# Rotary tables, projections, head-norm slices and gate rows set at other places in a two-block transformer kernel

## The chip, the cores and the metric

One core of one Trainium2 chip runs the whole program in one launch. The metric is the device time of that launch in microseconds (us); the time of the kernel before is a median of three runs. TensorE is called PE in the rows, VectorE DVE, ScalarE ACT, GpSimd POOL, and SP is the engine whose queue issues nearly all transfers.

## What is computed

512 tokens of width 1024 pass through two transformer blocks. The first has stick-breaking attention and latent (MLA) softmax attention with rotary positions, eight heads each, and then a mixture of 16,384 tiny experts. The second has a modulation computed from a vector `c` (called ada in the kernel), three kinds of attention heads (six "fox" heads with a forgetting gate, four mLSTM heads, six block-sparse "moba" heads) and a gated feed-forward layer. The parts that the change touches, cut from the reference:

```python
# first block
proj = h @ w_in[l]                      # sb_q, sb_k, sb_v, cq, ckv, k_pe
q = (rms_norm(cq, cq_norm[l]) @ w_uq[l]).reshape(b, s, MLA_HEADS, MLA_QK_DIM)
q = rms_norm(q, q_norm[l]); k = rms_norm(k, k_norm[l])
q = concatenate([q[..., :64], rope(q[..., 64:], positions)])   # cos and sin tables
# second block
mod = silu(c) @ w_ada[l] + b_ada[l]     # six rows: sh1, sc1, g1, sh2, sc2, g2
y_fox  = _fox_attention(_rms(fq, fox_q_g), _rms(fk, fox_k_g), fv, ff + fox_f_bias)
y_moba = _moba_attention(_rms(bq, moba_q_g), _rms(bk, moba_k_g), bv, slopes)
x = x + g1 * (y @ w_out[l])
x = x + g2 * ((silu(gate) * up) @ w_down[l])
```

## The kernel before

Tokens lie in four tiles of 128. Every fp32 product is made of three products of rounded parts ("a triple", `mm3`, lines 329 to 331): a weight tile is loaded on SP's queue (`w`), rounded by ACT (`whi`, line 198), and its remainder taken by DVE, for some weights by POOL (`wlo`, line 200). The stream `W` does this two weight tiles ahead of use: the call `W.get` that opens a weight tile puts the cast and the subtraction of a later tile into the queues of ACT and DVE.

Each engine runs its own list in the order in which the program was written; no scheduler reorders it. So what is written first also stands first in the queue, and a DVE instruction whose input is late holds up all DVE work behind it. The order is made by Python generators. `tok_gen` yields after each triple of a token product (32 triples for a full one), `feat_gen` after each triple of a 128-feature product (8 triples). `beside(main, side)` takes one step of `side` after each triple of `main`. `mix(main, fill)` and `Fill.run` hand out steps of a filler by a credit in ns. `run_pipe` lays out the attention items with lags between scores, transposes and value products, and gives the filler a credit for each item.

In order of time, what the change touches:

- **Tables.** After the products `cq` and `ckv`, DVE computes the rotary tables (lines 670 to 705, one sine on ACT), and then `latent_T` runs beside the product `sbv`: squares on ACT, a Newton inverse root on DVE, scaling, and transposes of `cqk` on PE (line 375).
- **Head norms.** `head_norm_gen` normalises and rotates the MLA queries `m_q` as a filler of the products `ukv` and `sbqk_gen(0)`; then `head_T` transposes them (line 768). The same is done for the keys `m_k` beside `sbqk_gen(1)` and `(2)`; `sbqk_gen(3)` is a filler of the attention.
- **Second block.** `fq` is projected, then `fk` with `fox_q` beside it, then `bq` with `fox_k` beside it. Each of these side generators holds a head norm of 16 steps (12 of the inverse root, 4 multiplications `fx_t`), then some small work, then transposes (line 1421). `moba_heads` does the same for `bq` and `bk`. `cum` is the running sum of the forgetting gates.
- **Ada.** On each `W.get`, one step of `ada_gen` loads a 128x512 piece of `w_ada`, multiplies it on POOL by a column of silu(c) broadcast along the row (lines 642, 644) and adds it (line 645). PE sums such a piece over partitions some steps later (line 633).
- **Gate rows.** `row_from_cols` turns the column form of `g1` and `g2` into rows: eight times DVE builds a diagonal `dg` and PE multiplies it by ones. For `g1r` this stands between the last transposes of `y` and the second half of the output product `out0`; for `g2r` between the last `up` product and the `down` product.

Of the kernel before, what the change touches and what calls it, by code (L numbers as in the profile page):

```python
# [15 lines left out]
OP = mybir.AluOpType  # L16
# [38 lines left out]
OUT_EARLY = 8  # L55

# [102 lines left out]
def build(tc, A, out):  # L159
# [459 lines left out]
    def ada_gen(pool, js):  # L619
# [16 lines left out]
        for i, (j, c) in enumerate(units):  # L636
            load(i + 1)
            w = tiles.pop(i)
            col_ = csil[:, c:c + 1].to_broadcast([P, 512])
            if c == 0:  # L640
                ac = pool.tile([P, 512], F32, name="ada_a", bufs=2)
                nc.gpsimd.tensor_tensor(ac, w, col_, op=OP.mult)
            else:
                nc.gpsimd.tensor_tensor(w, w, col_, op=OP.mult)
                nc.gpsimd.tensor_tensor(ac, ac, w, op=OP.add)
# [25 lines left out]
    nc.vector.memset(chmask[0:64, S - 64:S], NEG)  # L671
    nc.vector.tensor_scalar(utri, jp, 0.0, None, op0=OP.is_ge)
    posf = b1.tile([P, NT], F32, name="posf")
    nc.vector.tensor_copy(posf, posi)
    ang = b1.tile([P, 2, NT, 16], F32, name="ang")
    for tt in range(NT):
        nc.vector.tensor_scalar(ang[:, 0, tt, :], invf, posf[:, tt:tt + 1], None, op0=OP.mult)
    angk = b1.tile([P, 2, NT, 16], F32, name="angk")
    MAGIC = 12582912.0
    i2p = 1.0 / (2.0 * math.pi)  # L680
    nc.vector.tensor_scalar(angk[:, 0], ang[:, 0], i2p, MAGIC, op0=OP.mult, op1=OP.add)
    nc.vector.tensor_scalar(angk[:, 1], ang[:, 0], i2p, 0.25, op0=OP.mult, op1=OP.add)
    nc.vector.tensor_scalar(angk[:, 1], angk[:, 1], MAGIC, None, op0=OP.add)
    nc.vector.tensor_scalar(angk, angk, -MAGIC, None, op0=OP.add)
    nc.vector.tensor_copy(ang[:, 1], ang[:, 0])
    c1 = 6.28125
    c2 = float(np.float32(np.floor((2 * math.pi - c1) * 2 ** 20) / 2 ** 20))
    c3 = float(np.float32(2 * math.pi - c1 - c2))
    for cc in (c1, c2, c3):
        nc.vector.scalar_tensor_tensor(ang, angk, -cc, ang, op0=OP.mult, op1=OP.add)  # L690
    nc.vector.tensor_scalar(ang[:, 1], ang[:, 1], math.pi / 2, None, op0=OP.add)
    PI = 3.1415925
    nc.vector.tensor_scalar(ang, ang, PI, -PI, op0=OP.min, op1=OP.max)
    nc.scalar.activation(ang, ang, AF.Sin)

    trig = []
    for k, g in enumerate((qr, kr)):
        t = b1.tile([P, NT, 4, 16], F32, name="trig%d" % k)
        g1 = g[:, None, 0:16].to_broadcast([P, NT, 16])
        g2 = g[:, None, 16:32].to_broadcast([P, NT, 16])  # L700
        nc.vector.tensor_mul(t[:, :, 0, :], ang[:, 1], g1)
        nc.vector.tensor_mul(t[:, :, 1, :], ang[:, 1], g2)
        nc.vector.tensor_mul(t[:, :, 2, :], ang[:, 0], g2)
        nc.vector.tensor_scalar(t[:, :, 2, :], t[:, :, 2, :], -1.0, None, op0=OP.mult)
        nc.vector.tensor_mul(t[:, :, 3, :], ang[:, 0], g1)
        trig.append(t)

    sbv = b1.tile([P, NT, 512], F32, name="sbv", tag="sbv")
# [1073 lines left out]
```

## Time and profile before

| what | value |
|---|---|
| median of three runs | 2392.91 us (2389.0 to 2395.34) |
| the profiled execution | 2386.05 us, its span 2384.3 us |
| PE busy | 2272.4 us, 95% of the span |
| DVE, ACT, POOL busy | 1603.8, 967.2, 1085.2 us |
| mean granted clock of PE | 0.971 of full speed |

PE is the engine that is busy nearly all the time, so what counts is when it waits and at which clock it runs. A line of the timeline of PE begins with the start in us from the span's start and the duration; where PE was idle before, the idle time and what it waited for stand in brackets at the end. A row of stretches has, for each engine, the busy us and the number of instructions, then the granted clock (1.00 is 2.4 GHz, 0.50 is 1.2 GHz), the share of the transfer engines and GB/s.

### The profile page before, as it was taken

The page shows a single profiled execution, that of the slowest core. Times are in us where ns is not written, and L with a number is a line of the kernel's source. Part 1 is how long each engine was busy: PE and PEld are TensorE (multiplying, and loading weights), DVE is VectorE, ACT ScalarE, POOL GpSimd, SP SyncE. Part 2 cuts the span into 40 slices and gives each one's busy share as a digit, 9 for nine tenths or more (in the row PEclk, how much of TensorE's full clock was granted, in tenths as well). Part 3 has the DMA queues.
Part 4 walks back from the last instruction along what each step waited for, and adds up shares of the span by engine and source line. Part 5 has one row for each costly group of instructions (what it writes and reads, how often), then busy time and mean ns, then how long its engine had stood idle before and what let it go on. Part 6 is the DMA issues. An engine that isn't in the chain of part 4 may idle for free.

```text
span 2384.3 us, 31909 instructions
## 1 busy us (share of the span) xinstructions
PE 2272.4 (95%) x11721; PEld 1948.5 (82%) x11721; DVE 1603.8 (67%) x2979; ACT 967.2 (41%) x1712; POOL 1085.2 (46%) x763
## 2 busy tenths in 40 slices
PE   7899999988989999999999999999799998999999
PEld 7777778878878888888888888888797776888787
DVE  5666639999967788888888877875675355433322
ACT  4556633446763333333333333335454434222211
POOL 4460024645766666776667666643656102500000
PEclk9998999999999999999999999999899899999999
DMA  5430042325688888998989888962342112423231
GB/s 169 137 115 1 11 154 88 104 96 197 238 292 304 306 303 298 319 313 310 331 306 320 307 307 306 317 235 90 128 131 93 45 36 71 158 92 98 85 112 56
DMA packets 174936, 439.91 MB, mean 184 GB/s; under 512 B 16956, under 2 KB 71100, under 8 KB 171708
## 3 DMA queue, kind: packets, MB, share of 16 engines
q1 hardware_dynamic: 136188, 301.28, 37.6%
q0 software_dynamic: 36864, 134.23, 15.5%
q10 hardware_dynamic: 1728, 2.36, 0.3%
q8 instruction: 92, 1.51, 0.3%
q14 instruction: 64, 0.52, 0.1%
HBM read 406.10 MB, written 31.72 MB: 184 GB/s over the span
## 4 chain that ended last, share of the span: by engine, by line
PE 70%; DVE 15%; issue 5%; POOL 4%; ACT 3%; DMA 2%; SPq 0%; ACTq 0%; POOLq 0%; DVEq 0%
PE bank L331 20%; PE bank L329 20%; PE bank L330 20%; DVE ohAB L1114 3%; DVE ohA L1121 3%; PE bank L571 2%; POOL rows L1241 2%; PE bank L582 2%; POOL wlo L200 2%; PE bank L563 1%; DVE wlo L200 1%; DMA w<-in_uT_dram 1%; PE bank L811 1%; DVE eq L1054 1%; DMA w<-in_peer_v_dram 1%
## 5 line engine op out<-in xcount | busy, mean ns | idle before, releaser
L200 POOL TENSOR_TENSOR wlo<-w,whi 128x1024 fp32r<-128x1024 f32 (+2 forms) x154 | 398.4, 2590 | 416.8 <-ACT whi L198 367.9
L331 PE MATMUL bank<-hhi,wlo 128*128 128x384 f32 (+1 forms) x1600 | 576.0, 360 | 11.3 <-POOL wlo L200 10.9
L329 PE MATMUL bank<-hhi,whi 128*128 128x384 f32 (+1 forms) x1600 | 579.7, 362 | 0.7 <-ACT ge L914 0.7
L330 PE MATMUL bank<-hlo,whi 128*128 128x384 f32 (+1 forms) x1600 | 573.3, 358 | 1.4 <-DVE hlo L455 1.4
L198 ACT CAST whi<-w 128x1024 fp32r<-128x1024 f32 (+4 forms) x414 | 420.9, 1024 | 322.2 <-PE bank L331 173.8
L200 DVE TENSOR_TENSOR wlo<-w,whi 128x1024 fp32r<-128x1024 f32 (+2 forms) x260 | 326.9, 1259 | 277.3 <-ACT whi L198 275.4
L331 PEld LDWEIGHTS bank<-hhi,wlo 128*128 128x128 f32 x1600 | 303.5, 190 | 39.2 <-POOL wlo L200 16.3
L329 PEld LDWEIGHTS bank<-hhi,whi 128*128 128x128 f32 x1600 | 303.5, 190 | 34.1 <-issue 4.1
L330 PEld LDWEIGHTS bank<-hlo,whi 128*128 128x128 f32 x1600 | 303.4, 190 | 30.2 <-DVE hlo L455 2.0
L330 PE MATMUL bank<-wlo,ch 128*128 128x512 f32 x768 | 304.7, 397 | 4.5 <-DVE wlo L200 4.4
L329 PE MATMUL bank<-whi,ch 128*128 128x512 f32 x768 | 304.3, 396 | 4.3 <-DMA w<-in_uT_dram 2.8
L331 PE MATMUL bank<-whi,cl 128*128 128x512 f32 x768 | 304.4, 396 | 0.0
L1219 DVE TENSOR_TENSOR cl<-ge,ch 128x384 fp32r<-128x384 f32 x125 | 148.5, 1188 | 140.4 <-ACT ch L1218 139.5
L1241 POOL DMA_INDIRECT rows<-in_peer_v_dram,eidx x128 | 183.2, 1432 | 109.7 <-DVE acc L1264 81.8
L1241 POOL DMA_INDIRECT rows<-in_peer_u_dram,eidx x128 | 178.5, 1394 | 99.6 <-DVE junk L1259 75.3
L1259 DVE SCALAR_TENSOR_TENSOR junk<-rows,h 128x1024 bf16<-128x1024 f32 x128 | 188.3, 1471 | 0.5 <-DMA rows<-in_peer_u_dram,eidx 0.2
L1264 DVE SCALAR_TENSOR_TENSOR acc<-rows,coefg,acc 128x1024 f32<-128x1024 f32 x127 | 181.6, 1430 | 0.7 <-DMA rows<-in_peer_v_dram,eidx 0.4
L330 PEld LDWEIGHTS bank<-wlo,ch 128*128 128x128 f32 x768 | 144.8, 189 | 36.6 <-DVE wlo L200 5.3
L329 PEld LDWEIGHTS bank<-whi,ch 128*128 128x128 f32 x768 | 144.8, 188 | 36.2 <-ACT ch L1212 3.1
L331 PEld LDWEIGHTS bank<-whi,cl 128*128 128x128 f32 x768 | 144.9, 189 | 35.7 <-DVE cl L1219 0.6
L329 PE MATMUL bank<-whi,hhi 128*128 128x384 f32 (+3 forms) x448 | 170.5, 381 | 0.0
L914 ACT ACTIVATE ge<-bank 128x384 f32<-128x384 f32 x116 | 57.1, 493 | 269.8 <-PE bank L331 265.7
(384 smaller groups left out, 3553.5 us busy)
## 6 DMA issues: line engine op xcount, KB each, us to landing
w<-in_uT_dram SPq DMA_DIRECT2D x128, 512.0 KB
w<-in_peer_v_dram SPq DMA_DIRECT2D x128, 512.0 KB
ada_w<-in_w_ada_dram SPq DMA_DIRECT2D x96, 256.0 KB
gdram<-gs SPq DMA_DIRECT2D x24, 1024.0 KB
gblk<-gdram SPq DMA_DIRECT2D x16, 1536.0 KB
w<-in_w_gu_dram SPq DMA_DIRECT2D x44, 512.0 KB
w<-in_w_down_dram SPq DMA_DIRECT2D x22, 512.0 KB
w<-in_w_pq_dram SPq DMA_DIRECT2D x16, 512.0 KB
```

What stands on the lines that cost most here:

```text
L198: nc.scalar.copy(hi[:, :n], t[:, :n])
L200: (eng or nc.vector).tensor_tensor(lo[:, :n], t[:, :n], hi[:, :n].bitcast(F32), op=OP.subtract)
L329: nc.tensor.matmul(o, ah, bh, start=start, stop=False)
L330: nc.tensor.matmul(o, ah, bl, start=False, stop=False)
L331: nc.tensor.matmul(o, al, bh, start=False, stop=stop)
L914: nc.scalar.activation(t, b[:, :DTOK], AF.Gelu)
L1114: nc.vector.tensor_tensor(AB.rearrange("p c b i t -> p (c b) i t"), iota4, IJ[:, n].rearrange("p c (b t) -> p (c b) t", t=2).unsqueeze(2) ...
L1121: nc.vector.tensor_tensor(A[:, c], AB[:, 0], g_, op=OP.mult)
L1219: nc.vector.tensor_sub(cl, t, ch.bitcast(F32))
L1241: nc.gpsimd.indirect_dma_start(out=r, out_offset=None, in_=A["peer_" + kind], in_offset=bass.IndirectOffsetOnAxis(ap=eidx[:, k:k + 1], axi ...
L1259: nc.vector.scalar_tensor_tensor(junk, r, 1.0, h2, op0=OP.mult, op1=OP.mult, accum_out=preg[:, k:k + 1])
L1264: nc.vector.scalar_tensor_tensor(acc, r, coefg[:, k:k + 1], acc, op0=OP.mult, op1=OP.add)
```

## The change

It has five parts. The rotary tables become a generator, `tables()`, and run beside the `cq` product, one step after each triple. `sbqk_gen` can be called for its query or key half alone: the query half of 1 moves in front of the transposes of `m_q`, and the query half of 3 in front of those of `m_k`; within `head_norm_gen`, the rotation uses four instructions over all tokens instead of sixteen. In the second block `SLACK = 6` empty steps stand between the head norms and what follows. `row_from_cols` becomes `row_gen`, whose steps run beside the second half of `out0` for `g1r` and beside the `gate` product of the last but one slice (f = 20) for `g2r`. POOL multiplies in `ada_gen` by a per-partition scalar (`tensor_scalar`) instead of a broadcast tile.

```diff
@@ ada_gen
-            col_ = csil[:, c:c + 1].to_broadcast([P, 512])
+            col_ = csil[:, c:c + 1]
...
-                nc.gpsimd.tensor_tensor(w, w, col_, op=OP.mult)
+                nc.gpsimd.tensor_scalar(w, w, col_, None, op0=OP.mult)
                 nc.gpsimd.tensor_tensor(ac, ac, w, op=OP.add)
@@ tables
-    proj_tok("cq", hhi, hlo, KC, 384, lambda tt, b: nc.scalar.copy(cqk[:, tt, :384], b[:, :384]))
+    def tables():
+        nc.vector.memset(chmask, 0.0)
+        yield
...
+        nc.scalar.activation(ang, ang, AF.Sin)
+        yield
...
+    drain(beside(tok_gen("cq", hhi, hlo, KC, 384, lambda tt, b: nc.scalar.copy(cqk[:, tt, :384], b[:, :384])), tables()))
     proj_tok("ckv", hhi, hlo, KC, 288, ev_ckv)
-
-    nc.vector.memset(chmask, 0.0)
...
@@ sbqk_gen, head_norm_gen
-    def sbqk_gen(j):
+    def sbqk_gen(j, part=(0, 1)):
...
-            for tt in range(NT):
-                nc.vector.tensor_mul(tabs[k][:, tt], s4[:, tt, :, x0:x0 + 16],
-                                     tr[:, tt, k, :][:, None, :].to_broadcast([P, NH, 16]))
-            yield 800.0
+            nc.vector.tensor_mul(tabs[k], s4[:, :, :, x0:x0 + 16],
+                                 tr[:, :, k, :].unsqueeze(2).to_broadcast([P, NT, NH, 16]))
+            yield 700.0
...
     mix(sbqk_gen(0), fill)
+    mix(sbqk_gen(1, (0,)), fill)
     fill.finish()
     fill = Fill(head_norm_gen(ks, trig[1]))
     for tt in range(NT):
         head_T(tt, qs, qg, qhT)
-    mix(sbqk_gen(1), fill, 0.9)
+    mix(sbqk_gen(1, (1,)), fill, 0.9)
     mix(sbqk_gen(2), fill, 0.9)
+    mix(sbqk_gen(3, (0,)), fill, 0.9)
     fill.finish()
...
     def behind():
-        yield from sbqk_gen(3)
+        yield from sbqk_gen(3, (1,))
@@ second block
         def fox_q():
             yield from tq.norm()
+            for _ in range(SLACK):
+                yield
...
             for tt, t in enumerate(tk.t):
                 nc.vector.tensor_scalar(t[:, :, 64], cum[:, tt, 0:6], -8.0, None, op0=OP.mult)
-            yield
+                yield
+            for _ in range(SLACK - 3):
+                yield
             yield from fox_T(tk.t, fkg, kTf)
...
         def moba_heads(heads, gain, dst):
             yield from heads.norm()
+            for _ in range(SLACK):
+                yield
@@ gate rows
+    def row_gen(cols, pool, t):
+        b = dg = None
+        for k in range(9):
+            if k and k % 4 == 0:
+                nc.tensor.matmul(b[:, 384:512], ones, dg, start=True, stop=True)
+                nc.scalar.copy(t[:, (k - 4) * P:k * P], b)
+            elif k:
+                nc.tensor.matmul(b[:, (k - 1) % 4 * P:(k - 1) % 4 * P + P], ones, dg, start=True, stop=True)
+            if k == 8:
+                return
+            if k % 4 == 0:
+                b = bank()
+            dg = pool.tile([P, P], F32, name="dg", bufs=2)
+            nc.vector.tensor_scalar(dg, ident, cols[:, k:k + 1], None, op0=OP.mult)
+            yield
...
-        late_["pool"], late_["g1r"] = b3, row_from_cols(g1c, b3, "g1r")
-        drain(out0)
+        late_["pool"], late_["g1r"] = b3, b3.tile([P, D], F32, name="g1r")
+        drain(beside(out0, row_gen(g1c, b3, late_["g1r"])))
...
-                proj_feat(("gate", f), hhi, hlo, KC, ev_gate)
+                if f == NF - 2:
+                    drain(ada)
+                    W.tick = None
+                    row = row_gen(g2c, b4, g2r)
+                drain(beside(feat_gen(("gate", f), hhi, hlo, KC, ev_gate), row))
                 proj_feat(("up", f), hhi, hlo, KC, ev_up)
-        drain(ada)
-        W.tick = None
-        g2r = row_from_cols(g2c, b4, "g2r")
```

How the instructions move on DVE, at three places. First, behind the norm of the input (`hlo` is the last part of it), where `wlo` belongs to the products `cq` and `ckv` and `ang` to the tables. Before:

```order
L447 SCALAR_TENSOR_TENSOR hlo<-bank,c_attn_norm,hhi 128x512 x8
L200 TENSOR_TENSOR wlo<-w_95,whi 128x768
L200 TENSOR_TENSOR wlo<-w_188,whi 128x576
...
L200 TENSOR_TENSOR wlo<-w_396,whi 128x1024
L670 MEMSET chmask 128x512
...
L705 TENSOR_TENSOR trig_568<-ang,r_k_rope_g 128x4x16
L200 TENSOR_TENSOR wlo<-w_434,whi 128x1024
L335 TENSOR_SCALAR rs_v<-lt_595 128x4
```

The same place now:

```order
L449 SCALAR_TENSOR_TENSOR hlo<-bank,c_attn_norm,hhi 128x512 x8
L673 MEMSET chmask 128x512
...
L684 TENSOR_SCALAR ang<-invf,posf 128x16 x4
L202 TENSOR_TENSOR wlo<-w_95,whi 128x768
...
L703 SCALAR_TENSOR_TENSOR ang<-angk,ang 128x128 x3
L202 TENSOR_TENSOR wlo<-w_188,whi 128x576
...
L725 TENSOR_TENSOR trig_395<-ang,r_k_rope_g 128x4x16
L202 TENSOR_TENSOR wlo<-w_300,whi 128x576
```

The tables, which stood behind seven weight subtractions and in front of the inverse root `rs_v`, now stand between the first subtractions.

Second, beside the `fk` product: `fx_t` are the multiplications of the query norm of the fox heads, `cum` the gates' running sum that the transposes wait for, `hr_ss` the sums of squares of the keys that the product makes. Before:

```order
L1388 TENSOR_TENSOR fx_t<-fx_t,rs_r 128x6x64 x4
L200 TENSOR_TENSOR wlo<-w_15570,whi 128x768
L1443 MEMSET fx_t 128x6 x4
L1449 COPY cum<-bank 128x56
L1367 TENSOR_REDUCE hr_ss<-hr_sq 128x6 x4
```

The same place now:

```order
L1419 TENSOR_TENSOR fx_t<-fx_t,rs_r 128x6x64 x4
L202 TENSOR_TENSOR wlo<-w_15546,whi 128x768
L1398 TENSOR_REDUCE hr_ss<-hr_sq 128x6
L1476 MEMSET fx_t 128x6 x4
L1482 COPY cum<-bank 128x56
L1398 TENSOR_REDUCE hr_ss<-hr_sq 128x6 x3
```

One of the four reductions of the keys has moved in front of the memsets and of `cum`.

Third, where `g1r` is made: `hlo` ends the transposes of `y`, `wlo` belongs to the output product. Before:

```order
L1481 TENSOR_TENSOR hlo<-bank,hhi 128x512 x2
L1338 TENSOR_SCALAR dg<-ident,modc 128x128 x8
L200 TENSOR_TENSOR wlo<-w_17613,whi 128x1024
L200 TENSOR_TENSOR wlo<-w_17881,whi 128x1024
L1635 TENSOR_TENSOR o_t<-bank,g1r 128x512
```

The same place now:

```order
L1518 TENSOR_TENSOR hlo<-bank,hhi 128x512 x2
L202 TENSOR_TENSOR wlo<-w_17589,whi 128x1024
L1371 TENSOR_SCALAR dg<-ident,modc 128x128 x8
L202 TENSOR_TENSOR wlo<-w_17857,whi 128x1024
L1672 TENSOR_TENSOR o_t<-bank,g1r 128x512
```

A weight subtraction, which waits for a cast on ACT, now stands in front of the diagonals.

## Rows read from the trace of the kernel before

**Rows 1.** the page, its first part: busy time of TensorE and its share
```profile
PE 2272.4 (95%) x11721; PEld 1948.5 (82%) x11721; DVE 1603.8 (67%) x2979; ACT 967.2 (41%) x1712; POOL 1085.2 (46%) x763
```

**Rows 2.** timeline of PE: start, us, operation, [idle before <- releaser]
```profile
70.65 1.09 PE L375 MATMUL bank<-ident,cqk 128*128 128x128 f32 x4 [6.32 <-DVE cqk L369]
126.11 5.34 PE L768 MATMUL bank<-ident,m_q 128*96 128x128 f32 x32 [3.48 <-DVE m_q L760]
155.05 3.67 PE L768 MATMUL bank<-ident,m_k 128*96 128x128 f32 x32 [1.61 <-DVE m_k L760]
1690.38 1.09 PE L1421 MATMUL bank<-ident,fx_t 128*65 128x128 f32 x4 [7.88 <-DVE cum L1449]
1716.79 0.62 PE L1421 MATMUL bank<-ident,fx_t 128*65 128x128 f32 x4 [4.38 <-DVE fx_t L1456]
1949.63 4.40 PE L1339 MATMUL bank<-dg,ones 128*128 128x128 f32 x16 [1.75 <-DVE dg L1338]
2023.09 0.50 PE L331 MATMUL bank<-hhi,wlo 128*128 128x512 f32 x1 [2.52 <-POOL wlo L200]
2252.33 0.71 PE L1339 MATMUL bank<-dg,ones 128*128 128x128 f32 x4 [2.36 <-DVE dg L1338]
```

**Rows 3.** busy times by stretch; the granted clock stands behind POOL
```profile
70.00:74.00 4.00, 3.35 (x12) 2.98 (x13) 1.58 (x4) 1.55 (x4) 2.49 (x3) 0.50 0.52 174
180.00:190.00 10.00, 10.00 (x74) 8.53 (x74) 5.59 (x29) 7.48 (x23) 0.00 (x0) 1.00 0.01 2
1717.00:1722.00 5.00, 5.00 (x26) 4.74 (x25) 0.00 (x0) 2.68 (x6) 3.13 (x4) 0.66 0.36 109
2024.00:2032.00 8.00, 8.00 (x37) 6.56 (x36) 2.98 (x4) 1.57 (x2) 6.89 (x6) 1.00 0.83 295
```

**Rows 4.** timelines of DVE, then ACT, around the rotary tables
```profile
52.05 0.48 DVE L670 MEMSET chmask<- 128x512 f32 x1
...
60.18 0.22 DVE L705 TENSOR_TENSOR trig<-ang,r_k_rope_g 128x64 f32<-128x64 f32 x1
...
59.59 0.52 ACT L359 ACTIVATE junk<-cqk 128x384 bf16<-128x384 f32 x1
```

**Rows 5.** timeline of PE: starts of triples in 384- and 512-column products
```profile
35.17 0.34 PE L329 MATMUL bank<-whi,hhi 128*128 128x384 f32 x1
...
35.70 0.34 PE L329 MATMUL bank<-whi,hhi 128*128 128x384 f32 x1
...
52.27 0.39 PE L329 MATMUL bank<-whi,hhi 128*128 128x512 f32 x1
...
52.97 0.40 PE L329 MATMUL bank<-whi,hhi 128*128 128x512 f32 x1
```

**Rows 6.** timeline of DVE: the multiplications of the head norms
```profile
120.35 2.50 DVE L756 TENSOR_TENSOR hn_t<-m_q,trig 128x128 f32<-128x128 f32 x12
...
1684.03 4.46 DVE L1388 TENSOR_TENSOR fx_t<-fx_t,rs_r 128x384 f32<-128x384 f32 x3
...
1709.03 4.76 DVE L1388 TENSOR_TENSOR fx_t<-fx_t,rs_r 128x384 f32<-128x384 f32 x4
...
1747.81 0.56 DVE L1388 TENSOR_TENSOR fx_t<-fx_t,rs_r 128x384 f32<-128x384 f32 x1
```

**Rows 7.** timelines of ACT, DVE and PE around the two gate rows
```profile
1954.55 1.05 ACT L198 CAST whi<-w 128x1024 fp32r<-128x1024 f32 x1
...
1955.63 1.23 DVE L200 TENSOR_TENSOR wlo<-w,whi 128x1024 fp32r<-128x1024 f32 x1 [2.15 <-ACT whi L198]
...
2256.23 0.76 PE L329 MATMUL bank<-whi,ahi 128*128 128x512 f32 x1
```

**Rows 8.** groups of POOL by form: xcount | busy, mean ns | idle before
```profile
L645 POOL TENSOR_TENSOR ada_a<-ada_a,ada_w 128x512 f32<-128x512 f32 x84 | 126.1, 1501 | 6.6
L644 POOL TENSOR_TENSOR ada_w<-ada_w,c_c 128x512 f32<-128x512 f32 x84 | 109.3, 1301 | 125.8 <-DMA ada_w<-in_w_ada_dram 125.5
...
L1352 POOL IOTA dist<- 128x512 f32 x1 | 0.6, 558 | 4.1 <-DVE hlo L455 4.1
```

More of the change, by code (lines that the diff above doesn't have):

```diff
@@ L55 @@
 OUT_EARLY = 8
+SLACK = 6
 NPRE = 4
@@ L678, in build @@
[L678 to L706, printed above, removed]
+    trig = []
@@ L726, in build @@
     qk = {}
-    def sbqk_gen(j):
-        qk[j] = b1.tile([P, 2, S], F32, name="sbqk", tag="qk%d" % j)
-        yield from feat_gen(("sbq", j), hhi, hlo, KC, lambda b: nc.scalar.mul(qk[j][:, 0, :], b, 0.125))
-        yield from feat_gen(("sbk", j), hhi, hlo, KC, lambda b: nc.scalar.copy(qk[j][:, 1, :], b))
+    def sbqk_gen(j, part=(0, 1)):
+        if 0 in part:
+            qk[j] = b1.tile([P, 2, S], F32, name="sbqk", tag="qk%d" % j)
+            yield from feat_gen(("sbq", j), hhi, hlo, KC, lambda b: nc.scalar.mul(qk[j][:, 0, :], b, 0.125))
+        if 1 in part:
+            yield from feat_gen(("sbk", j), hhi, hlo, KC, lambda b: nc.scalar.copy(qk[j][:, 1, :], b))
     qhT = b1.tile([96, NH, S], F32, name="qhT")
@@ L1328, in build @@
     pst.close()
-    def row_from_cols(cols, pool, name):
-        t = pool.tile([P, D], F32, name=name)
-        for hh in range(2):
-            b = bank()
-            for k in range(4):
-                dg = pool.tile([P, P], F32, name="dg", bufs=2)
-                nc.vector.tensor_scalar(dg, ident, cols[:, hh * 4 + k:hh * 4 + k + 1], None, op0=OP.mult)
-                nc.tensor.matmul(b[:, k * P:(k + 1) * P], ones, dg, start=True, stop=True)
-            nc.scalar.copy(t[:, hh * 512:(hh + 1) * 512], b)
-        return t
+    def row_gen(cols, pool, t):
[12 more added lines that the diff above has]
+            nc.vector.tensor_scalar(dg, ident, cols[:, k:k + 1], None, op0=OP.mult)
+            yield
     with tc.tile_pool(name="nrm", bufs=1) as nrm:
@@ L1441, in fox_q @@
             yield from tq.norm()
+            for _ in range(SLACK):
+                yield
             for t in tq.t:
@@ L1456, in fox_k @@
                 nc.vector.tensor_scalar(t[:, :, 64], cum[:, tt, 0:6], -8.0, None, op0=OP.mult)
-            yield
+                yield
+            for _ in range(SLACK - 3):
+                yield
             yield from fox_T(tk.t, fkg, kTf)
@@ L1462, in moba_heads @@
             yield from heads.norm()
+            for _ in range(SLACK):
+                yield
             yield from moba_T(heads.t, gain, dst)
@@ L1684, in build @@
         W.tick = ada_tick
+        row, g2r = iter(()), b4.tile([P, D], F32, name="g2r")
         for f in range(NF):
```

54 lines of the change are left out of this document (46 added, 8 removed).

## The prediction

> **What bounds the kernel now.** I read the busy times first: PE works 95% of the span [rows 1], so a change can gain only where PE stands still, or works at the low clock. The second view was the timeline of PE, searched for idle time above 0.4 us in the stretches that the change touches. The waits that it aims at are seven, and their releasers name the work in front of them [rows 2]: 6.32 us for the scaled latents `cqk`, 3.48 and 1.61 for the rotated queries and keys, 7.88 for `cum` and 4.38 for `fx_t` at the fox heads, 1.75 and 2.36 for the diagonals of the gate rows. They sum to 27.8 us. An eighth, 2.52 us for a `wlo` that POOL makes, stands behind ada work on POOL.
>
> The third view was the granted clock by stretches [rows 3]. Behind the 6.32 us wait PE runs at 0.50, that is 1.2 GHz, for the whole of 70 to 74 us; behind the 4.38 us wait the mean over 5 us is 0.66; behind the 2.52 us wait it is 1.00. So a long wait costs something after its end as well, and one of about 2.5 us need not. Products go at 0.53 us a triple (384 columns) and 0.70 us (512) at 2.4 GHz [rows 5].
>
> **The tables.** DVE spends 52.05 to 60.40 on them, and ACT, which must do the sine in between, starts the squares of the latents at 59.59 [rows 4]. These eight microseconds delay everything that the transposes of `cqk` wait for. Beside `cq` the same instructions stand between weight subtractions that have time: the product lasts 32 x 0.53 = 17 us, and DVE is asked there for 8.4 us of tables and a few subtractions of about 1 us each. If that cover failed, the late subtractions would hold up `cq` or `ckv` by a few us at most, the bound on the bad side. The sine stands in front of the evictions of `cq` on ACT, whose banks are not needed at once. Now the squares can start when the last latent is evicted: about 52.3 by the place where DVE's tables began, and one cast of 1.05 us [rows 7] ahead of them, so 53.3 in place of 59.59, 6.3 us earlier. The transposes would be ready at 70.65 - 6.3 = 64.4; PE reaches them at 70.65 - 6.32 = 64.3. About half a microsecond of wait is left, for a small cast and subtraction that stand in front of the scaling. Gain 5.8 us, and the half-speed stretch goes with it: 4 us at 0.50 are 2.0 us of lost work. Sum 7.8; bounds 4 (2 us of wait left, the clock unchanged) and 8.3.
>
> **The projections.** Eight triples of 0.70 us, 5.6 us, move in front of the transposes of `m_q`. They use finished operands, and the filler of the head norm is fully written out before them, so DVE's end of `m_q` doesn't move; 5.6 covers the 3.48 us. The 32 transposes then last 3.67 us, as for `m_k`, not 5.34 [rows 2]. Gain 5.2. For the keys the number of triples between the two groups of transposes stays 8 + 16 + 8 = 32, so nothing more is hidden there; the four larger rotations instead of sixteen (2.50 us for twelve [rows 6]) may save about 1 us, and transposes that end earlier than their evictions on ACT take about as much back. I put 0 for the keys, between -1.5 and +1.6. The triples taken from the attention's filler are no loss if PE is full there without them: from 180 to 190 us the filler is used up and PE is busy 10.00 of 10 [rows 3]. If it weren't, 5.6 us at most would come back; I take 0.
>
> **The slack.** Six empty steps let PE do six more triples, 6 x 0.53 = 3.2 us, before it asks for the transposes. For the queries that is 1690.38 - 7.88 + 3.2 = 1685.7. DVE is ready at 1690.38 before; now a reduction over 384 columns (about 0.56 us, like a multiplication of that size [rows 6]) stands in front of `cum`, so 1690.9. The wait shrinks from 7.88 to 5.2, a gain of 2.6, and the clock behind it stays low. What makes DVE late is contention: three `fx_t` take 4.46 us where one alone takes 0.56 [rows 6]. POOL runs ada work all that time, at 1.30 us a multiplication and 1.50 an addition [rows 8].
>
> The Trainium skill, "SBUF — State Buffer", section "Who interferes with whom", says that a DVE instruction with two SBUF inputs and a GpSimd instruction that reads SBUF exclude each other, one waiting for the whole of the other. The 4.46 us against 3 x 0.56 agree. By that rule the new POOL multiplication, which reads SBUF too, still locks DVE out, only for a shorter time, so that slack alone can't free the chain.
>
> How long a POOL multiplication by a scalar takes no row shows. The nearest rows are IOTA, 512 columns that are only written, 0.56 us, and the addition with two full inputs, 1.50; the old one took 1.30 [rows 8]. I take 1.0, closer to the old form, whose second input is one column read again and again: 0.3 us less for each of about five DVE instructions that wait behind one here, 1.5 us. The bounds are 5 x 0.74 = 3.7 better and 5 x 0.20 = 1.0 worse. The Trainium skill, "GPSIMD Engine Reference", section "Performance versus the Vector engine", gives 1.03 cycles an element for a body with one input; my estimate from that page is 0.44 us for 512 columns, by which the queries' wait would lose 4.3 us in place of 1.5.
>
> For the keys the wait is 4.38, the steps cover 3.2, and nothing new stands in front: 1.2 is left, short enough to keep the clock, where 5 us at 0.66 lost 1.7 before [rows 3]; I count 1.5 of these. Gain 4.7, bounds 1 and 6.1. The `moba` norms run inside the attention, where no wait of PE names them: 0. Since the steps shift the end of the fox transposes, one more eviction and square on ACT come before the first exponential: -1.
>
> **The gate rows.** `g1r` takes PE from 1949.63 - 1.75 = 1947.9 to about 1954.0 [rows 2], 6.1 us with nothing else. Beside `out0` two triples (1.4 us) come first, and then PE asks for the first `dg`. But the `W.get` in front has put a cast and a subtraction before it: from the cast's start to the end of `wlo` 2.3 us [rows 7]; it can start about 0.6 us after 1947.9, so `dg` is there at 1951.0 and PE has waited 1.8 us since 1949.3. The eight products themselves cost 1.7 us (0.71 us for two at the low clock [rows 2], so about 0.2 each). Gain 6.1 - 1.8 - 1.7 = 2.6. `g2r` takes from 2252.33 - 2.36 = 2249.97 to 2256.23 [rows 2, 7], 6.3 us. Now its first `dg` stands behind the last remainder of `up`, as before, and behind a cast and a subtraction too: I get 2.5 us of wait after two triples, then 1.7. Gain 2.0. Together 4.6; bounds -0.5 (both waits pull the clock down) and 8.7 (no wait). The 2.52 us for POOL's `wlo` has two ada multiplications in front: 0.5, from -0.5 to 2.
>
> **The sum.** 7.8 + 5.2 + 2.6 + 1.5 + 4.7 - 1 + 4.6 + 0.5 = 25.9, say 26 us. The profiled execution took 2386.05 (span 2384.3), so its like would take 2360. It lay 6.9 us under the median of the runs, 2392.91; on the median's scale I predict 2367.
>
> **Rivals.**
> 1. *The waits move with the work.* DVE is in order, so a late DVE chain stays late whatever PE does meanwhile. For it speaks that at the fox queries 5.2 of 7.88 us stay even by my own sum, and that both `dg` get a new wait; against it that tables and projections have their cover on paper. Then tables 7.8 and projections 3.5 hold, the keys of fox give 2, the rest 0: 13 us, 2380.
> 2. *POOL's lock shrinks most of all.* If the multiplication comes near IOTA's 0.56, the queries lose 3.7 instead of 1.5, the keys their last 1.2, the POOL `wlo` 2 and the clock behind the queries returns 1.7: 33 us, 2360.
> 3. *Slower, by POOL.* If the scalar form is slow, ada falls behind. Each `ada_w` piece holds one of two buffers, its load stands in SP's queue in front of the next weight load, and PE waits for weights. The old multiplication has 125.8 us of idle time in front of 84 of them [rows 8], 1.5 us each, so nothing is seen up to 1.3 + 1.5 = 2.8 us. The 26 us are given back at 2.8 + 26/84 = 3.1 us; at 3.4 the loss is 0.6 x 84 = 50 us, net 24 slower, 2417. Against it: it would have to be twice as slow as the addition with two inputs.
> 4. *Nothing in the end.* What PE saves is taken back by stretches at the low clock at other places, where no wait shows: 52 us at 0.50 would do it; 2393.
>
> **How the numbers follow.** Forecast 0.53, rival 1 0.20, rival 2 0.17, rival 3 0.04, rival 4 0.06. No change means within 0.3% of the median, 7.2 us, about what a measurement of this kernel can tell. Cases 0, 1 and 2 are all faster: 0.90, of which I give 0.01 to no change: 0.89, 0.07, 0.04. The range reaches from 39 us gained (rival 2 and the better bounds of the tables and rows) to 11 us gained (rival 1 with a weaker projection term), 2354 to 2382. The spread of the median, 3 us to either side, is in it.
>
> **What would show it.** Right: squares on ACT begin near 53 us, the wait for `cqk` is under 1 us and the clock behind it 1.00; no wait above 1 us before `m_q`, about 1.5 before `m_k`; 4 to 5 us before the first fox transposes of the queries, about 1 before those of the keys; about 2 us in front of the first `dg` of either row, with products following at full speed; POOL's multiplication at about 1.0 us. Wrong: a `cq` or `ckv` triple that waits for `wlo`, gaps in the attention after 165 us, a multiplication on POOL above 2.8 us, or half-speed stretches without a wait in front.

## The result and the profile after

The changed kernel takes 2352.15 us (median of 4 runs, 2348.34 to 2388.42) against 2390.95 us for the kernel before: ratio 0.9828 [0.9802, 0.9854]. Forecast were 2367 us, range 2354 to 2382. The gain is about 39 us by the medians instead of 26 (41 by the ratio, 37 by the ratio of the second comparison below). In some executions, among them the first profiled ones of the changed kernel (2388.42 us) and of the tables put back (2389.76 us), PE runs at 0.50 from about 220 to 300 us and the time is some 35 us longer: ratios leave out executions more than 1.5% above the fastest of their kernel while medians hold all, the rows of the changed kernel are from a second execution (2346.07 us, span 2344.3 us), and those of the tables put back are read only up to 80 us.

The page of that execution, its first part, answers to [rows 1]:

```profile
PE 2256.7 (96%) x11721; PEld 1939.6 (83%) x11721; DVE 1588.4 (68%) x2955; ACT 964.1 (41%) x1712; POOL 1122.6 (48%) x763
```

POOL is busy 37 us longer than before, with the same number of instructions. The timeline of PE at the places of [rows 2], and one wait more (`mlo`, in the first attention) (the line numbers of the changed kernel are its own):

```profile
65.37 0.68 PE L377 MATMUL bank<-ident,cqk 128*128 128x128 f32 x4 [0.66 <-DVE cqk L371]
121.08 3.65 PE L791 MATMUL bank<-ident,m_q 128*96 128x128 f32 x32
147.69 3.67 PE L791 MATMUL bank<-ident,m_k 128*96 128x128 f32 x32 [0.96 <-DVE m_k L783]
218.81 1.45 PE L377 MATMUL bank<-ident,mlo 128*128 128x128 f32 x5 [3.85 <-DVE mlo L371]
1664.33 0.60 PE L1452 MATMUL bank<-ident,fx_t 128*65 128x128 f32 x4
1684.71 0.60 PE L1452 MATMUL bank<-ident,fx_t 128*65 128x128 f32 x4
1914.08 0.46 PE L1365 MATMUL bank<-dg,ones 128*128 128x128 f32 x2 [1.83 <-DVE dg L1371]
1983.71 0.50 PE L333 MATMUL bank<-hhi,wlo 128*128 128x512 f32 x1 [2.51 <-POOL wlo L202]
2194.04 0.49 PE L1365 MATMUL bank<-dg,ones 128*128 128x128 f32 x2 [2.46 <-DVE dg L1371]
```

The reader is to see four things. The waits for `cqk`, `m_k` and both `dg` stand at 0.66, 0.96, 1.83 and 2.46 us, close to the 0.5, 1.6, 1.8 and 2.5 of the forecast. Both fox transposes start without a wait that the timeline shows, where 5.2 and 1.2 us were forecast. And POOL's `wlo` is waited for as long as before. The wait for `mlo` at 218.81 us is new: a gap in the attention after 165 us was one of the signs of being wrong.

The squares of the latents begin where the forecast put them (53.3). Timeline of ACT:

```profile
53.45 0.54 ACT L361 ACTIVATE junk<-cqk 128x384 bf16<-128x384 f32 x1
```

Stretches, with the clock behind POOL, as [rows 3]: behind `cqk`, behind the fox queries, behind POOL's `wlo`:

```profile
66.00:70.00 4.00, 3.71 (x21) 2.75 (x19) 2.43 (x4) 2.86 (x5) 3.48 (x4) 1.00 0.26 94
...
1665.00:1673.00 8.00, 8.00 (x55) 7.73 (x54) 1.66 (x3) 7.35 (x15) 7.45 (x6) 1.00 0.51 164
...
1984.00:1992.00 8.00, 8.00 (x29) 6.40 (x29) 1.43 (x2) 0.61 (x2) 7.48 (x5) 0.79 0.82 266
```

And here is the surprise, the forms of POOL that answer to [rows 8] (xcount | busy, mean ns | idle before):

```profile
L646 POOL TENSOR_SCALAR ada_w<-ada_w,c_c 128x512 f32<-128x512 f32 x84 | 151.6, 1805 | 82.2 <-DMA ada_w<-in_w_ada_dram 81.9
L647 POOL TENSOR_TENSOR ada_a<-ada_a,ada_w 128x512 f32<-128x512 f32 x84 | 114.3, 1361 | 7.0
```

The multiplication became longer, 1.80 us in place of 1.30, and yet the chains on DVE that compete with it became shorter. The multiplications `fx_t` of the head norms, minimum/median/maximum in ns, in the kernel before and then in the changed one:

```profile
L1388 DVE TENSOR_TENSOR fx_t<-fx_t,rs_r x16: 554/1391/1659, 1683.6 to 1780.0; 128x384 f32<-128x384 f32 x16
```

```profile
L1419 DVE TENSOR_TENSOR fx_t<-fx_t,rs_r x16: 545/553/1650, 1659.7 to 1741.6; 128x384 f32<-128x384 f32 x16
```

### The profile page after: what moved, and what is told of

Same layout as the page of the kernel before. It is cut to its first block, busy times and chain, and to the rows that moved or that the text cites. A ratio compares the mean times of both kernels' runs of the same rounds, so it can differ in the third digit from the quotient of the medians.

```text
span 2386.7 us, 31873 instructions
## 1 busy us (share of the span) xinstructions
PE 2295.7 (96%) x11721; PEld 1963.7 (82%) x11721; DVE 1591.5 (67%) x2955; ACT 966.3 (40%) x1712; POOL 1124.4 (47%) x763
## 4 chain that ended last, share of the span: by engine, by line
PE 76%; DVE 12%; issue 3%; ACT 3%; POOL 3%; DMA 2%; SPq 0%; ACTq 0%; POOLq 0%; DVEq 0%
PE bank L331 21%; PE bank L333 21%; PE bank L332 21%; PE bank L573 3%; DVE ohAB L1139 3%; DVE ohA L1146 3%; PE bank L584 2%; POOL rows L1266 2%; PE bank L565 2%; PE bank L836 1%; POOL wlo L202 1%; DMA w<-in_uT_dram 1%; DMA w<-in_peer_v_dram 1%; DVE eq L1079 1%; PE bank L1018 1%
## 5 line engine op out<-in xcount | busy, mean ns | idle before, releaser
L202 DVE TENSOR_TENSOR wlo<-w,whi 128x1024 fp32r<-128x1024 f32 (+2 forms) x260 | 316.2, 1218 | 263.5 <-ACT whi L200 263.3
L646 POOL TENSOR_SCALAR ada_w<-ada_w,c_c 128x512 f32<-128x512 f32 x84 | 151.6, 1804 | 79.1 <-DMA ada_w<-in_w_ada_dram 78.7
```

The costliest lines, as they stand in the source:

```text
L202: (eng or nc.vector).tensor_tensor(lo[:, :n], t[:, :n], hi[:, :n].bitcast(F32), op=OP.subtract)
L646: nc.gpsimd.tensor_scalar(w, w, col_, None, op0=OP.mult)
```

## The experiments

Two theories for the 13 us that were not forecast. A: POOL's scalar form, though longer, holds DVE up less, and the chains at the fox heads are done earlier. B: the clock of PE in the attention, or chance in one of the executions. The table cuts the span at starts of PE's instructions: the norm behind the first attention, the norm that opens the second block, the first 4-row transposes of `mT` (early in the second attention, so that the third stage holds all fox transposes), the last eight value products, the norm behind `out0`. Each number is a difference of two starts, in us.

One execution of each kernel stands in the table, so the scatter must be known. Executions whose program is the same in a stage, those of the later experiments included, gave 316.5 to 319.8 us in the first block, 1286.8 to 1296.8 among the experts, 152.7 to 153.7 from the second block to `mT`, 142.3 to 148.7 in the second attention and 392.2 to 394.8 in the rest. The stage to `mT` is the one in which a difference of a few us can be read from single executions.

| stage | before (two executions) | changed | POOL form back | POOL form alone | no slack | diagonals ahead |
|---|---|---|---|---|---|---|
| first block | 330.9, 331.9 | 318.1 | 322.8 | 328.0 | 316.5 | 319.8 |
| experts | 1296.8, 1290.5 | 1287.1 | 1289.3 | 1288.9 | 1288.5 | 1287.9 |
| second block to `mT` | 168.3, 171.5 | 153.6 | 163.5 | 161.2 | 160.2 | 152.9 |
| second attention | 142.6, 142.7 | 142.8 | 142.7 | 146.6 | 142.6 | 146.6 |
| to the norm behind `out0` | 52.8, 54.1 | 50.5 | 50.5 | 52.8 | 50.5 | 48.5 |
| rest | 392.9, 394.6 | 392.2 | 394.1 | 393.0 | 392.2 | 391.1 |

**The changed kernel again.** No edit.

> The changed kernel itself once more, for a second profile and a closer ratio. Measured so far: 2348 to 2353 us, ratio 0.983, 39 us gained where 26 were summed. Theory A (POOL): the extra gain sits at the fox heads; the wait for the query transposes is gone entirely (5.2 us were expected to stay) because DVE's four fx_t take about 2 us in place of 4.94. Theory B (clock): the extra gain sits in the attention of the first block; this profile then shows 1.00 over most of 210 to 300 us, with under 5 us lost to the low clock where the kernel before lost about 7 (0.62 and 0.52 over 220:240). Ratio 0.981 to 0.985 by either.

Measured: 2350.75 us, ratio 0.9846 [0.9819, 0.9873]. Theory A's picture is there: four `fx_t` in 2.38 us, no wait for the queries. B's is there in part: 0.84 and 0.65 over 210 to 230, some 5 us lost where the kernel before lost about 9 (0.62 and 0.52 from 220 to 240). But the new wait of 3.85 us for `mlo` stands in the same place, so nothing of the 13 us is left for B there.

**POOL's form put back.**

```diff
-            col_ = csil[:, c:c + 1]
+            col_ = csil[:, c:c + 1].to_broadcast([P, 512])
-                nc.gpsimd.tensor_scalar(w, w, col_, None, op0=OP.mult)
+                nc.gpsimd.tensor_tensor(w, w, col_, op=OP.mult)
```

> The changed kernel with one part undone: POOL multiplies by the broadcast column again. Theory A: fx_t on DVE is back at 1.2 to 1.4 us each, the wait before the first query transposes is 4 to 6 us, and the kernel is 6 to 11 us slower than the changed one (ratio to the kernel before 0.986 to 0.989). Theory B: within 3 us of the changed one (0.983 to 0.985). My prediction's own term (1.5 us for this part) lies with theory B here.

Measured: 2363.44 us, 0.9878 [0.985, 0.9907], about 8 us over the changed kernel by the ratios, whose intervals overlap. So the whole does not tell the two kernels apart; the stages do. The waits come back, though the queries' by less than A expected, and one at the MLA keys that nobody had named:

```profile
151.95 4.47 PE L791 MATMUL bank<-ident,m_k 128*96 128x128 f32 x20 [4.24 <-DVE m_k L783]
...
1673.93 1.09 PE L1452 MATMUL bank<-ident,fx_t 128*65 128x128 f32 x4 [2.37 <-DVE fx_t L1476]
1699.44 0.62 PE L1452 MATMUL bank<-ident,fx_t 128*65 128x128 f32 x4 [2.24 <-DVE fx_t L1489]
```

Of the table, 9.9 us lie in the stage to `mT`, ten times its scatter, and 4.6 in the first block (3.0 above the longest of the executions with the changed program), where ada work runs on POOL too. The expected 1.2 to 1.4 us for each `fx_t` failed: their median is 0.61, since the queries' four met POOL at a good moment. It is the whole chain that counts: from `rs_v` to `cum` 12.0 us with this form and slack, 9.4 with the scalar form; in the kernel before 13.4 and 12.5.

**POOL's form alone**, in the kernel before. The same two lines the other way round.

> The kernel before with this part alone: POOL multiplies by a per-partition scalar. Theory A: POOL's multiplication takes 1.55 us or more instead of 1.04 to 1.30, and yet the four fx_t take about 2 us, the 7.88 us wait falls to 4 to 5, the 4.38 us wait to 2 to 3, and the kernel gains 4 to 9 us (ratio 0.996 to 0.998). Theory B: 0 to 2 us (0.999 to 1.000). If the longer multiplication held up ada and through it the weights, it would be slower than before.

Measured: 2371.61 us, 0.9923 [0.9895, 0.995], a gain of 18 us (12 to 25), above what either theory gave. The waits of 7.88 and 4.38 us fall to:

```profile
1674.01 1.09 PE L1421 MATMUL bank<-ident,fx_t 128*65 128x128 f32 x4 [2.43 <-DVE cum L1449]
1697.35 0.62 PE L1421 MATMUL bank<-ident,fx_t 128*65 128x128 f32 x4 [1.42 <-DVE fx_t L1456]
```

The stage to `mT` becomes 8.7 us shorter (against the mean of the two executions before; 7.1 against the shorter of them), the first block 3.4, which is as much as its scatter.

**The pairs by themselves.** Behind the end of the changed kernel: 8 POOL instructions of 512 columns and 16 DVE instructions of 384 columns, alone and together.

```diff
+        for dv, po in ((None, ps), (None, pb), (None, pf), (d2, None), (d1, None),
+                       (d2, ps), (d2, pb), (d2, pf), (d1, ps), (d1, pb), (d1, pf)):
...
+            for i in range(8):
+                if po:
+                    po(i)
+                if dv:
+                    dv(i)
+                    dv(i)
```

> The changed kernel with a measurement added behind its end (so its time is longer by 100 to 200 us and means nothing): 8 POOL instructions of 512 columns alone in each of three forms (scalar, broadcast column, two full inputs), 16 DVE instructions of 384 columns alone (two inputs, one input), then each of the six pairs together. Theory A: the two-input DVE instruction keeps its 0.5 us beside the scalar form, and takes over 1 us beside both others, which exclude it. Theory B, which takes the rule that any POOL instruction reading SBUF excludes it: over 1 us beside all three forms, longest beside the one that lasts longest, the scalar form. One-input DVE instructions: unchanged beside all forms by both.

One line's instructions in each stretch, minimum/median/maximum in ns. L1767 is POOL's scalar form, L1770 the broadcast column, L1773 two full inputs; L1761 is DVE with two inputs, L1764 with one. Where the two engines worked together, only the instructions are counted that ran while the other engine was at work: DVE has 16 of them in a stretch and POOL 8, so a part of either list runs alone. DVE with two inputs alone, then beside L1767, L1770, L1773; with one input the same; POOL's three forms, each alone and then beside L1761:

```profile
L1761 DVE TENSOR_TENSOR mb_dc<-mb_da,mb_db x16: 550/558/559, 2385.3 to 2394.2; 128x384 f32<-128x384 f32 x16
L1761 DVE TENSOR_TENSOR mb_dc<-mb_da,mb_db x14: 557/559/930, 2402.3 to 2411.5; 128x384 f32<-128x384 f32 x14
L1761 DVE TENSOR_TENSOR mb_dc<-mb_da,mb_db x8: 1277/1278/1279, 2418.4 to 2427.5; 128x384 f32<-128x384 f32 x8
L1761 DVE TENSOR_TENSOR mb_dc<-mb_da,mb_db x8: 1499/1499/1501, 2433.6 to 2444.3; 128x384 f32<-128x384 f32 x8
L1764 DVE TENSOR_SCALAR mb_dc<-mb_da x16: 359/360/361, 2394.8 to 2400.7; 128x384 f32<-128x384 f32 x16
L1764 DVE TENSOR_SCALAR mb_dc<-mb_da x14: 359/640/751, 2450.2 to 2458.4; 128x384 f32<-128x384 f32 x14
L1764 DVE TENSOR_SCALAR mb_dc<-mb_da x8: 1078/1082/1083, 2465.2 to 2473.1; 128x384 f32<-128x384 f32 x8
L1764 DVE TENSOR_SCALAR mb_dc<-mb_da x8: 1302/1305/1306, 2477.3 to 2486.7; 128x384 f32<-128x384 f32 x8
L1767 POOL TENSOR_SCALAR mb_pc<-mb_pa,c_c x8: 1562/1562/1584, 2351.0 to 2362.7; 128x512 f32<-128x512 f32 x8
L1767 POOL TENSOR_SCALAR mb_pc<-mb_pa,c_c x5: 1952/1973/1997, 2401.7 to 2409.9; 128x512 f32<-128x512 f32 x5
L1770 POOL TENSOR_TENSOR mb_pc<-mb_pa,c_c x8: 1038/1038/1038, 2364.9 to 2372.7; 128x512 f32<-128x512 f32 x8
L1770 POOL TENSOR_TENSOR mb_pc<-mb_pa,c_c x8: 1232/1235/1444, 2417.8 to 2427.2; 128x512 f32<-128x512 f32 x8
L1773 POOL TENSOR_TENSOR mb_pc<-mb_pa,mb_pb x8: 1259/1262/1262, 2374.4 to 2383.7; 128x512 f32<-128x512 f32 x8
L1773 POOL TENSOR_TENSOR mb_pc<-mb_pa,mb_pb x8: 1455/1456/1675, 2433.0 to 2444.0; 128x512 f32<-128x512 f32 x8
```

This settles it for two inputs. The scalar form is the longest alone (1.56 us against 1.04 and 1.26), but beside it most DVE instructions keep their 0.56: one in three, five of the fourteen, takes 0.85 to 0.93. Beside the other two forms each of the eight takes 1.28 or 1.50, and POOL gets in one instruction for each of DVE's. So a POOL instruction costs DVE about 0.29 us in its scalar form, 0.72 with a broadcast column and 0.94 with two full inputs, while POOL itself becomes longer by 0.41, 0.20 and 0.19. Theory A's "keeps" is not exact, and theory B's order is wrong. What both said of one-input instructions failed: from 0.36 us they go to 1.08 and 1.31 beside the broadcast and the two full inputs, and beside the scalar form two in three are longer, 0.64 and 0.74.

**The kernel before again.** No edit.

> The kernel before, unchanged, for a second profile of it. In the first one the stage of the experts (from the norm behind the first attention to the norm that opens the second block) took 1296.8 us, in the changed kernel and in both variants so far 1287.1 to 1289.3, with the same program in it. Theory A: 8 us of that difference are the scatter of one execution, and the second profile shows 1287 to 1291 there. Theory B: the stage really starts otherwise in the kernel before (order of transfers, clock at entry), and it is above 1294 again.

Measured: 2386.93 us; the experts took 1290.5 us, theory A. In the last experiment below, which holds all of the change, the same stage took 1296.1 us. So it scatters by 9 us and more from one execution to the next, and nothing of it is put down to the change.

**No slack.**

```diff
-SLACK = 6
+SLACK = 0
...
-                yield
-            for _ in range(SLACK - 3):
-                yield
+            yield
```

> The changed kernel without its empty steps between head norms and transposes (SLACK 0, the keys' steps as before). My prediction's terms for the slack are 2.6 us (queries) and 4.7 us (keys). If these stand with POOL's scalar form in place: 5 to 8 us slower than the changed kernel. If POOL's form has already freed DVE, as the kernel before with that form alone shows (waits 2.43 and 1.42 us): 3 to 5 us slower, with waits of about 2.4 and 1.4 us at the fox heads. If DVE's chain sets the end there whatever PE does meanwhile: no difference.

Measured: 2362.38 us, 0.9892 [0.9868, 0.9916], 11.6 us over the changed kernel by the medians, 6.6 us at the fox heads by the table. The waits are 1.77 and 1.66 us, and the clock is 0.50 from 1663 to 1667 and from 1697 to 1701 us, where the changed kernel keeps 1.00 from 1620 us to `mT`:

```profile
1662.62 0.62 PE L1452 MATMUL bank<-ident,fx_t 128*65 128x128 f32 x4 [1.77 <-DVE cum L1482]
...
1686.37 0.62 PE L1452 MATMUL bank<-ident,fx_t 128*65 128x128 f32 x4 [1.66 <-DVE fx_t L1489]
```

**Diagonals four steps ahead.** The products lag, and for `g2r` the diagonals lie in the ring `d_t` over the gate and the up product.

```diff
-        for k in range(9):
+        for k in range(8 + LAG):
+            q = k - LAG
...
+                nc.tensor.matmul(b[:, q % 4 * P:q % 4 * P + P], ones, dgs[q], start=True, stop=True)
```

> The changed kernel with the diagonals of the gate rows built four steps ahead of their products (for the second row in the ring of the last eviction tiles, over the gate and the up product). If the waits of 1.83 and 2.46 us come from the subtraction that stands in front of the first diagonal, as predicted: both gone, 4 us faster than the changed kernel (ratio to the kernel before 0.982 to 0.984). If the diagonals themselves are late on DVE, or the waits only move to the next triple: no difference.

Measured: 2347.79 us, 0.9826 [0.9794, 0.9858]. The wait of `g1r` is gone and the stage shorter by 2.0 us; that of `g2r` is 0.41:

```profile
2198.54 0.49 PE L1366 MATMUL bank<-d_t,ones 128*128 128x128 f32 x2 [0.41 <-DVE d_t L1376]
```

So the subtraction in front of the first diagonal was the reason. As a whole the two kernels are not told apart.

**A gate for `mlo`.**

```diff
...
+        yield lambda: step["k"] >= 41
...
```

> The changed kernel with one gate more in the filler of the first attention: the transposes of the MLA output wait until item 41, not 38 as their norm. If the wait of 3.85 us for mlo is PE asking too early (the filler has 8 triples less than before, so PE gets there sooner): it goes, and with it the stretch at 0.65 to 0.84 behind it; 4 to 8 us faster than the changed kernel. If DVE's chain of items sets the pace of the attention: the wait spreads over the following items and the time stays within 2 us.

Measured: 2349.52 us, 0.984 [0.9815, 0.9865], the wait for `mlo` at 3.85 us as it was. Item 41 was past when the norm was written out, so the order of PE and DVE did not change. This run says nothing of either theory; it is one more measurement of the changed kernel. A later one sets the gate at item 44.

**The tables put back.**

```diff
-    drain(beside(tok_gen("cq", hhi, hlo, KC, 384, ...), tables()))
+    proj_tok("cq", hhi, hlo, KC, 384, ...)
     proj_tok("ckv", hhi, hlo, KC, 288, ev_ckv)
+    drain(tables())
```

> The changed kernel with the rotary tables back behind the second latent product. My prediction's term is 7.8 us (5.8 of wait, 2.0 of half clock behind it); the trace of the changed kernel gives 5.2 to 6 for the wait (from 58.9 to 53.2 to 54.6 us between the first transposes of the input and those of cqk) and 1.5 to 2.4 for the transposes behind it. If the term is right: 6 to 8 us slower than the changed kernel (ratio 0.986 to 0.988), with a wait of 5 to 6 us for cqk. Rival: later stages take up the delay, less than 3 us slower.

Measured: 0.988 [0.9852, 0.9908], against 0.9846 about 8 us, but the intervals overlap. Its profiled execution shows the wait at 4.88 us; up to the end of the `cqk` transposes it needs 4.8 us more than the changed kernel (65.4 and 60.6 us from the first transposes of the input).

**The projections put back.**

```diff
-    mix(sbqk_gen(1, (0,)), fill)
...
-    mix(sbqk_gen(1, (1,)), fill, 0.9)
+    mix(sbqk_gen(1), fill, 0.9)
...
-    mix(sbqk_gen(3, (0,)), fill, 0.9)
...
-        yield from sbqk_gen(3, (1,))
+        yield from sbqk_gen(3)
```

> The changed kernel with the moved halves of the projections put back (the four larger rotations stay). My prediction's term is 5.2 us, all of it at the queries. If it is right: 4 to 7 us slower (ratio 0.986 to 0.988), with a wait of 3 to 4 us for m_q and transposes of 5.3 us instead of 3.7. Rival: the attention has lost filler and waits 3.85 us for mlo, so that half of the gain comes back when the filler does: 0 to 3 us slower, and no wait for mlo.

Measured: 2358.51 us, 0.9909 [0.9866, 0.9952]; the first block takes 322.1 us, 3.9 more than in the changed kernel. `m_q` is waited for 2.81 us, and `mlo` not at all. But the transposes of `m_q` last 3.7 us here, not 5.3. The 3.9 us lie between what the term and what its rival gave (4 to 7, 0 to 3), and 322.1 is only 2.3 above the longest first block of the changed program; the interval of the whole reaches over both. So the run does not decide. Nor is the missing wait for `mlo` a sign for the rival alone: the clock in front of it fell to 0.51 from 210 to 220 us, so PE was slower on the way to it.

**Diagonals ahead, and the gate at item 44.**

```diff
...
+        yield lambda: step["k"] >= 44
...
```

> The changed kernel with the diagonals of the gate rows four steps ahead (as in the run before) and the transposes of mlo held until item 44 of the first attention (item 41 had left the order of PE as it was). If the 3.85 us wait for mlo is PE asking too early: it is gone, the clock stays at 1.00 around 220 us, 4 to 8 us in the first attention and 2 to 4 us at the rows: 2341 to 2346 us, ratio 0.979 to 0.982. If the attention is paced by DVE and ACT: the wait spreads over the items, and 2346 to 2349 us remain.

Measured: 2349.06 us, 0.986 [0.9817, 0.9903]. No wait for `mlo`, and no gain: the first block takes 320.3 us, and the clock in the attention is lower than with the wait. Stretches, the changed kernel and then this one:

```profile
210.00:220.00 10.00, 6.10 (x33) 3.95 (x32) 7.46 (x26) 5.65 (x16) 0.00 (x0) 0.84 0.01 2
220.00:230.00 10.00, 10.00 (x48) 7.26 (x46) 6.62 (x11) 6.47 (x15) 0.00 (x0) 0.65 0.00 0
```

```profile
210.00:220.00 10.00, 9.92 (x37) 6.66 (x38) 8.06 (x26) 5.57 (x16) 0.00 (x0) 0.53 0.01 2
220.00:230.00 10.00, 10.00 (x34) 6.31 (x35) 5.55 (x13) 5.03 (x14) 0.00 (x0) 0.50 0.00 0
```

Wait and lost clock together are about 9 us with the wait and 10 without it. The same exchange stands in the execution of the pairs, whose program is that of the changed kernel up to its end. There is no wait for `mlo`, the clock is low earlier, and the first block takes 317.8 us against 318.1:

```profile
200.00:210.00 10.00, 9.49 (x49) 6.28 (x49) 6.39 (x17) 6.75 (x20) 0.00 (x0) 0.81 0.01 2
210.00:220.00 10.00, 10.00 (x37) 6.74 (x36) 7.60 (x25) 5.63 (x15) 0.00 (x0) 0.50 0.00 0
220.00:230.00 10.00, 10.00 (x49) 7.26 (x48) 6.43 (x13) 6.01 (x13) 0.00 (x0) 0.67 0.00 0
```

The kernel before, whose attention has the longer filler, has no such wait either, and the low clock:

```profile
210.00:220.00 10.00, 9.60 (x60) 6.35 (x58) 6.14 (x19) 7.77 (x21) 0.00 (x0) 1.00 0.00 1
220.00:230.00 10.00, 9.78 (x39) 6.58 (x39) 7.04 (x23) 6.07 (x19) 0.00 (x0) 0.62 0.01 2
230.00:240.00 10.00, 10.00 (x38) 7.00 (x37) 7.26 (x18) 6.26 (x13) 0.00 (x0) 0.52 0.00 0
```

Over the executions with `mlo` at its old place, eight of the nine with the shorter filler wait 3.85 us for it and none of the four with the longer one.

**Diagonals ahead, and the second slices' remainders on DVE.**

```diff
-        eng = nc.gpsimd if f < 2 else None
+        eng = nc.gpsimd if f < 1 else None
...
```

> The changed kernel with the diagonals of the gate rows four steps ahead and one line more: the weights of the second gate and up slices have their remainders made by DVE, not POOL. Every version so far has waited 2.5 us there for wlo from POOL, with 0.83 to 0.94 of the clock in the 20 us behind it. If the wait is POOL's queue (two ada multiplications at 1.56 us and an addition stand in front): it goes, and 3 to 4 us with it; with the diagonals' 2 to 4 us the kernel gains 4 to 7 us on the changed one (2343 to 2346 us, ratio 0.980 to 0.982). If the cast on ACT in front of both is late: DVE waits as POOL did, and 2347 to 2349 us stay.

Measured: 2351.04 us, 0.9866 [0.9818, 0.9915]. POOL's queue was the reason: no wait is left there, and the last stage takes 384.6 us in place of 391.1 and 388.4 (diagonals ahead alone, and with the gate) and 392.2 (changed kernel). The whole does not show it: the ratio is above the 0.9826 of the diagonals alone, and the intervals overlap. In the profiled execution the experts took 1296.1 us, 9 more than in the changed kernel. No version is shown to beat the changed kernel.

## Why the prediction was wrong

**The step that failed** is POOL's multiplication under "The slack": "I take 1.0 ... 0.3 us less for each of about five DVE instructions that wait behind one here, 1.5 us", with bounds from 1.0 worse to 3.7 better. Both ends rest on the assumption that DVE loses what POOL's instruction lasts. It does not. The instruction came out longer than even the bad bound (1.56 us alone, 1.80 in the mean, against 1.50), which would have meant a loss, and yet what it costs a two-input DVE instruction fell from 0.72 to 0.29 us. The term was also counted at the queries alone, with nothing for the keys and the first block. Measured was a gain of 8.7 us at the fox heads with the form alone: the queries' wait went from 7.88 and 6.74 us (the two executions before) to 2.43, the keys' from 4.38 and 5.44 to 1.42. Beside the slack it was 9.9, and in the first block 3.4 and 4.6, of which the scatter there, 3.3 us, leaves little certain.

The Trainium skill, "SBUF — State Buffer", section "Who interferes with whom", on whose rule I let slack be unable to free the chain, says that a DVE instruction with two SBUF inputs and a GpSimd instruction that reads SBUF contend. The broadcast and the two-input form agree (1.28 and 1.50 us for 0.56). The scalar form agrees in part: it reads SBUF as well, but holds up one DVE instruction in three, by 0.29 us of its own 1.56, and the measurement decides. The estimate of 0.44 us that I drew from the Trainium skill, "GPSIMD Engine Reference", section "Performance versus the Vector engine", stands against 1.56 measured.

**Tables**, 7.8: with POOL's old form the stretch up to the end of the `cqk` transposes shrinks from 67.8 and 68.8 to 61.0 us, 6.8 to 7.8 us. The term held. With the scalar form in place the same edit is worth about 5 there, because that form shortens the wait by itself: alone it needs 65.5 us for the stretch.

**Projections**, 5.2 and 0 for the keys: the wait for `m_q` is gone and its transposes last 3.65 us, as forecast. But two things that I put at nothing were not nothing. With the old form the keys wait 4.24 us where 1.61 and 0.91 stood, and in eight of the nine executions with the shorter filler the attention waits 3.85 us for `mlo`. I had read PE as full from a row of 180 to 190 us; the wait lies at 215 to 219. What it costs is open, since the clock is low for longer where it is missing. Tables and projections together, with the old form, gave 8.6 us in the first block (331.4 to 322.8) where 13.0 were summed; the scalar form brought the rest, 318.1.

**Slack**, 2.6 + 4.7 - 1 = 6.3: measured 6.4 us with the old form and 6.6 with the new, to `mT`. The sum held, by luck: its parts did not. With the old form the queries gained about 4.3 us (2.6 forecast), the keys 2.0 (4.7), and behind the keys' transposes, where -1 was forecast, the difference was 0.1 (all against the mean of the two executions before, with the six moved triples counted at 3.2 us).

**Gate rows**, 4.6: the two waits came as forecast (1.83 and 2.46 us). `g1r` gave 2.3 to 3.6 us for 2.6. `g2r`, forecast 2.0, is lost in the last stage's scatter of 2.6 us. **POOL's `wlo`**, 0.5: nothing, 2.51 us as before. In front of it the two multiplications are longer (1.56 each for 1.04 and 1.49 us) and the addition is shorter (1.44 for 2.23). The clock behind it, 1.00 in the row that I read, was 0.82 behind the same wait in the second execution of the kernel before and 0.79 in the changed kernel.

**The rivals.** Rival 1 is out as a whole: the waits did not move with the work, except for `mlo` and, with POOL's old form, for the MLA keys. Rival 2 was the nearest by its time, 2360, and by its place. Its title came true, POOL's lock shrank most of all; its condition did not, since the chain was freed by an instruction that is longer, not shorter. Rival 3's price never came, with a multiplication of 1.80 us below its point of 2.8. Rival 4 did not happen, though the half-clock stretches in both attentions are there in every version.

What stays open: by the ratios the form is worth 18 us alone (12 to 25) and about 8 in the changed kernel (not clear of noise), while the stage to `mT` and the first block account for 12.1 and 14.5. With stages that scatter by 6 and 10 us by themselves, these are not told apart; the 8.7 and 9.9 us at the fox heads are clear of that stage's scatter. Why the scalar form holds DVE up for a shorter time no run shows.

## What to carry to other kernels

The duration of an instruction on one engine does not say what it costs another: here the longer one (1.56 for 1.04 us) cost DVE less (0.29 for 0.72). Before such an instruction is replaced, measure the pair, each alone and both together, and count only what ran while both were at work: a median over the whole stretch mixes the two. Where a stage's chains hang on a shared resource, an edit elsewhere changes what each other edit is worth; here the tables were worth 7 us with one form and 5 with the other. And removing a wait of PE in a stretch where the clock falls anyway gave nothing back here.

## What the runs showed of the hardware

- POOL's multiplication of 128x512 by a per-partition scalar takes 1.56 us alone, by a broadcast column 1.04, an addition of two full tiles 1.26. Beside the first, two of three two-input DVE instructions keep their 0.56 us, the third takes 0.85, and POOL goes to 1.97. Beside the broadcast column each takes 1.28 and beside two full inputs 1.50, and POOL goes to 1.24 and 1.46.
- DVE instructions with one input, 0.36 us alone, take 1.08 beside POOL's broadcast form and 1.31 beside two full inputs; beside the scalar form two of three take 0.64 and 0.74. The Trainium skill, "SBUF — State Buffer", section "Who interferes with whom", frees them only outside the modes that use both ports; whether these ran in such a mode no run shows.
- In the attention of the first block the clock is 0.62 and 0.52 in the mean from 220 to 240 us in the kernel before, where PE had been 96% busy or more, and 0.84 and 0.65 from 210 to 230 around a wait of 3.85 us in the changed one. Where that wait was missing, by an edit or in another execution, it was low for longer (0.53 and 0.50; 0.81, 0.50 and then 0.67 from 200 to 230).
